# A hybrid block on one core: early sums of the first weight pair, later ring loads and residual adds, output matmuls tied to the last head, and a norm's row that moves

## The chip, the cores and the metric

The kernel runs on one core of a Trainium2 chip. The metric is the device time of one execution in microseconds. The kernel before took 2224.24 us at the median of three runs (2223.49 to 2225.36).

## The reference

One transformer-like block over 512 tokens with a model width of 2048, all in f32:

```
u = rmsnorm(h, attn_norm_w)
z, xbc, dt_raw, q, kc, vc, ks, vs, kw, vw, gate_raw = split(u @ w_in)
y_ssd = ssd_mixer(z, xbc, dt_raw, ...)          # chunked state space, 16 heads
y_att = nsa_mixer(q, kc, vc, ks, vs, kw, vw, gate_raw, ...)   # 16 heads, 4 KV heads
h = h + concat([y_ssd, y_att]) @ w_out
v = rmsnorm(h, ffn_norm_w)
h = h + (silu(v @ w_gate) * (v @ w_up)) @ w_down   # inner width 5632
out = rmsnorm(h, final_norm_w)
```

The attention adds three branches per head: compressed tokens, selected blocks and a window. With 512 tokens there are 8 selection blocks, so every causal block is selected, and the window covers everything too.

## The kernel before, in words

**Precision.** Every operand of a large product is split into a high and a low part: ScalarE casts the high part (`a_hi`, L139), VectorE subtracts it from the f32 value for the low part (`lo`, L142), and TensorE makes three matmuls (a triple) for a pair of operands. A block of weights thus needs a DMA, a cast, a subtract and then its triples.

**Stages.** Times are those of the profiled execution. To about 320 us, `w_in` is read in units (L278 to L280: one unit is a block of 128 columns over k, 512 tokens wide) and the SSD runs beside it. From there to about 770 us the attention heads run, with further units and the first half of `w_out` between them. The attention half of `w_out` follows: columns c=0 and c=1 as units (NOA = 2, `late` for c=1), then c=2 to c=15 as steps (L1419 to L1421) of 8 triples until 857 us. From 857 to 1738 us come 22 pairs of gate and up blocks (NP = 22), each as seven products in the manner of Strassen (M1 to M7). From 1740 us the down product runs in 35 visits (`VISITS`: column group j and a number of pairs n), each with seven products over its n pairs; visits 4 to 13 are at 1773 to 1940 us. The last 56 us are the final norm and the output.

**What orders the work.** The first part is generators under a scheduler that ticks once per triple (`sch.tick`); `yield 10` in a generator waits for ten ticks. Engines run their instructions in the order in which they were issued; `tc.issue_after(x)` pins an instruction behind x. The order of the second part is written out by hand: loads are issued in the order of the list `loads` as soon as slots are free (`advance`, L1331 issues them on SyncE's queue), sums of blocks are made by VectorE (L148), by GpSimd, or by a DMA that accumulates onto the loaded block (`plus`, L1333 on GpSimd's queue), and casts and subtracts run ahead of their triples.

**Places in memory that matter here.** Z and A hold loaded blocks (A has 8 slots), R and E the high and low parts. A lies where attention keeps k, the gates and the split weights of units, so its first writer has to wait until the last unit with attention's output is done. `SR`, a tile inside A's space, held the row of the FFN's norm (`srow`). Columns c=0 and c=1 of `w_out` stand in the list of loads as ghosts: they are not loaded, but take slots in Z.

**Sums for the first pair.** A product needs 11, 12, 22 or one of the sums S1 to S4 of the four blocks of gate (or up). For pair 0 the kernel loads five blocks a side with two accumulating DMAs, and VectorE makes four more sums of 128x1024.

**The ring.** For the down stage the product of gate and up for each pair lies in DRAM in seven forms (`g_d`, 1792 KB a unit), and comes back into a ring of eight slots (GRING = 8). `feed` (L1800 to L1818) issues one load at a time on ScalarE's DMA queue: a whole unit (L1811), or for slot 7 seven pieces of 256 KB (L1814). It issues unit n once `done[n - 8]` lies two steps back, and not faster than one unit per 7 us of the planned time. The first eight units have no predecessor, so they are issued as soon as the pace allows. Units 6 and 7 are first read in visit 8. A DMA of SyncE's or ScalarE's queue signals on one of eight semaphores in turn, and waits for the DMA that used that semaphore last.

**The residual.** h lies in DRAM in eight pieces (`h_d`); `add_h(j)` (L1819) adds piece j onto the output tile of column group j with an accumulating DMA of 512 KB on GpSimd's queue, in visit j+1.

Of the kernel before, what the change touches and what calls it, by code (L numbers as in the profile page):

```python
# [129 lines left out]
def body(ctx, tc, xT, w_in, w_out, w_gate, w_up, w_down, w1k, w1v, cols, rows, kst, out):  # L130
# [38 lines left out]
    def ps_m():  # L169
# [36 lines left out]
    class Unit:  # L206
        def __init__(self, src, nk, rhs, evac, need=(), pre=None, cols=(0, 512)):
            self.cols, self.rhs, self.evac, self.need, self.pre, self.nk = cols, rhs, evac, need, pre, nk
            self.hook, self.late = None, False
# [57 lines left out]
    def run_sub(u, p, sub):  # L267
        i, k0, n = sub
        issue_low(i)
        for j in range(n):  # L270
            if j == 0:
                issue_split(i + LEAD)
            if j == 2:
                issue_low(i + LEAD)
            k = k0 + j
            ah, al = [t[:, u.cols[0]:u.cols[1]] for t in u.rhs(k)]
            with tc.issue_after(R["pv"].ins) if u.late else nullcontext():
                pe.matmul(p, hi_t[i][:, j, :], ah, start=(k == 0), stop=False)  # L278
                pe.matmul(p, hi_t[i][:, j, :], al, start=False, stop=False)  # L279
                pe.matmul(p, lo_t[i][:, j, :], ah, start=False, stop=(k == u.nk - 1))  # L280
            sch.tick()
            if u.hook:
                u.hook(k)
# [368 lines left out]
    def ev_kc(g):  # L652
# [296 lines left out]
    def attention():  # L949
# [45 lines left out]
        def norm2(g, h, br, i):  # L995
            L = 128 * (i + 1)
            e, m = pr[g, h, br, i]
            if not br:
                a_hi(e[:, 0:L], e[:, 0:L], scale=m[:, 3:4])

        def trans(g, h, br, i):
            e, m = pr[g, h, br, i]
# [4 lines left out]
            for kb in range(i + 1):  # L1007
                pe.transpose(p[:, kb * 128:(kb + 1) * 128], e[:, kb * 128:(kb + 1) * 128], ident)
            pr[g, h, br, i] = p[:, 0:128 * (i + 1)].rearrange("p (a b) -> p a b", b=128)
# [9 lines left out]
        def pvmm(g, h, br, i):  # L1019
# [12 lines left out]
            for kb in range(4):  # L1032
                for t in (th, tl):
                    rhs = t[:, 4 * kb:3 * kb + 4, :].rearrange("p a b -> p (a b)")
                    R["pv"] = pe.matmul(o[:, kb * 128:512], v[:, kb, br, :], rhs, start=False,
                                        stop=(br == 1 and kb == 3 and t is tl))
        def out_a(g, h, br, i):
            if br == 1 and i == 3:
# [190 lines left out]
    for c in range(NOA):  # L1229
        units.append(Unit(w_out[c][:, 8:16, :], 8, ma_rhs, ev_head(c)))  # L1230
        units[-1].late = c >= 1

    class Blk:
# [11 lines left out]
        def read(self):  # L1248
            self.reads -= 1
            if not self.reads:  # L1250
                self.zone.free(self.at, self.n)
                self.at = None
# [55 lines left out]
    def advance():  # L1308
        while nxt["raw"] < len(loads):
# [3 lines left out]
            if b.inplace:  # L1313
# [116 lines left out]
    def pre_oa():  # L1430
# [47 lines left out]
    def ev_oa(c):  # L1478
        def ev(p):
# [218 lines left out]
    for u in range(NP):  # L1698
        for side, w in ((0, w_gate), (1, w_up)):
            qs[u, side] = quad(w[u], 0, 8)  # L1700

    loads += [qs[0, side][a] for a, side in (("11", 0), ("11", 1), ("S1", 0), ("12", 0), ("12", 1), ("S1", 1), ("S3", 0),
                                             ("22", 0), ("S3", 1), ("22", 1))]
    seq = [(0, M1), (1, M1), (0, M2), (1, M2), (0, M3), (1, M3)] + [(i, p) for i in range(2) for p in (M6, M7, M5, M4)]
    af0 = {0: gu_after(0, 0), 1: gu_after(0, 1)}
    bk0 = {0: banks(), 1: banks()}
    for n, (side, p) in enumerate(seq):
# [248 lines left out]
    for v, (j, a, b) in enumerate(visits):  # L1956
# [35 lines left out]
        else:  # L1992
            add_loads(q, "11 12 S2 S4 S3 22 S1" if "S4" in made else "11 12 S1 S3 22" if made else "11 12 21 22 S1 S3")
            af, bk = d_after(j, a == 0, b == NP, (j, b) == visits[-1][:2]), banks(BANK_D)
            for n, p in enumerate(SEQ_D):
                blk, sums = q["form"][p]
                s = Step(blk, g_rhs(p, a), bk(p), after=af(p), before=down_before(v, n) if v <= NJ else None, sums=sums)
        done.update((i, s.i) for i in range(a, b))

    def run_rest():  # L2000
# [177 lines left out]
```

## Time and profile before

| what | value |
|---|---|
| median of 3 runs | 2224.24 us |
| profiled execution | 2224.6 us |
| its span | 2222.7 us |
| mean granted TensorE clock | 0.993 |
| TensorE busy | 2172.0 us (98%) |
| VectorE busy | 1771.1 us (80%) |
| ScalarE busy | 1097.8 us (49%) |
| GpSimd busy | 431.1 us (19%) |
| mean DMA rate | 199 GB/s |

All times in the views are from the start of the span. The profile puts an instruction's wait in brackets with what released it; matmuls overlap, so the time between two starts says more than a duration. TensorE is called PE, VectorE DVE, ScalarE ACT, GpSimd POOL and SyncE SP; a q behind the name is that engine's DMA queue.

### The profile page before, as it was taken

What the parts mean: (1) busy time and instruction counts of PE and PEld (TensorE: products, weight loads), DVE (VectorE), ACT (ScalarE), POOL (GpSimd) and SP (SyncE); (2) the same over time, 40 slices, a digit from 0 to 9 for tenths busy, and PEclk for the clock granted to TensorE, in tenths of its full rate; (3) what the DMA queues carried; (4) which work ended last, traced back from release to release, by engine and by line L of the source; (5) the groups of instructions that cost most, each with busy time, mean ns of one, the idle gap of its engine ahead of it and who ended that gap; (6) DMA issues with size and microseconds to landing.
All of it is one profiled execution on the core that took longest, in us unless ns stands there. A gap on an engine that the chain in (4) does not pass through costs nothing. (4 is left out here: it accounts for less than half of the span.)

```text
span 2222.7 us, 39887 instructions
## 1 busy us (share of the span) xinstructions
PE 2172.0 (98%) x15407; PEld 2031.0 (91%) x15407; DVE 1771.1 (80%) x2876; ACT 1097.8 (49%) x1785; POOL 431.1 (19%) x457
## 2 busy tenths in 40 slices
PE   9999999999999899999999999999999999999996
PEld 7888888888888778999999999999999889999996
DVE  6799777788788677888887888888888757787886
ACT  5554457567666544444444444444444443333354
POOL 0012243333133053111111112100000002212121
PEclk9999999999999999999999999999999999999998
DMA  6222443222434176989999999987886988878776
GB/s 204 88 74 67 145 151 105 72 87 84 168 120 149 38 249 165 277 250 260 267 291 264 261 266 265 288 229 222 242 213 217 335 234 260 265 231 274 216 186 175
DMA packets 166607, 442.01 MB, mean 199 GB/s; under 512 B 17952, under 2 KB 32688, under 8 KB 166416
## 3 DMA queue, kind: packets, MB, share of 16 engines
q1 hardware_dynamic: 101872, 256.10, 33.2%
q0 software_dynamic: 32512, 91.73, 21.5%
q10 hardware_dynamic: 32032, 91.63, 11.8%
q8 instruction: 121, 1.98, 0.4%
q14 instruction: 70, 0.57, 0.1%
HBM read 375.95 MB, written 79.63 MB: 205 GB/s over the span
## 5 line engine op out<-in xcount | busy, mean ns | idle before, releaser
L139 ACT ACTIVATE R<-Z 128x1024 fp32r<-128x1024 f32 (+5 forms) x471 | 429.9, 933 | 526.4 <-DVE Z L148 283.3
L142 DVE TENSOR_TENSOR R<-Z,R 128x1024 fp32r<-128x1024 f32 (+5 forms) x365 | 373.9, 1031 | 51.8 <-ACT R L139 38.1
L278 PE MATMUL ps_g<-u,whi 128*128 128x512 f32 x736 | 292.1, 397 | 0.4 <-ACT pth L139 0.4
L280 PE MATMUL ps_g<-u,wlo 128*128 128x512 f32 x736 | 290.4, 395 | 0.0
L279 PE MATMUL ps_g<-u,whi 128*128 128x512 f32 x736 | 289.5, 393 | 0.2 <-DVE u L142 0.2
L1419 PE MATMUL ps_s<-u,R 128*128 128x256 f32 (+1 forms) x753 | 217.3, 289 | 1.7 <-ACT R L139 1.7
L1420 PE MATMUL ps_s<-u,R 128*128 128x256 f32 (+1 forms) x753 | 216.6, 288 | 0.0
L1419 PE MATMUL ps_g<-u,R 128*128 128x256 f32 (+1 forms) x751 | 214.7, 286 | 0.0
L1420 PE MATMUL ps_g<-u,R 128*128 128x256 f32 (+1 forms) x751 | 214.2, 285 | 0.0
L1419 PE MATMUL ps_t<-u,R 128*128 128x256 f32 (+1 forms) x699 | 201.0, 287 | 0.0
L1420 PE MATMUL ps_t<-u,R 128*128 128x256 f32 (+1 forms) x699 | 200.6, 287 | 0.0
L142 DVE TENSOR_TENSOR wlo<-wraw,whi 128x512 fp32r<-128x512 f32 x200 | 156.2, 783 | 49.2 <-ACT whi L139 48.4
L1421 PE MATMUL ps_g<-u,R 128*128 128x256 f32 (+1 forms) x623 | 179.1, 288 | 1.9 <-DVE R L142 1.8
L139 ACT ACTIVATE whi<-wraw 128x512 fp32r<-128x512 f32 x200 | 124.9, 627 | 111.4 <-PE ps_g L279 78.8
L1421 PE MATMUL ps_s<-u,R 128*128 128x256 f32 (+1 forms) x601 | 172.0, 286 | 2.1 <-DVE R L142 2.0
L280 PEld LDWEIGHTS ps_g<-u,wlo 128*128 128x128 f32 x736 | 138.4, 188 | 27.1
L279 PEld LDWEIGHTS ps_g<-u,whi 128*128 128x128 f32 x736 | 138.4, 188 | 26.8 <-DVE u L142 0.5
L278 PEld LDWEIGHTS ps_g<-u,whi 128*128 128x128 f32 x736 | 138.5, 188 | 26.4 <-ACT e L139 0.8
L1419 PEld LDWEIGHTS ps_s<-u,R 128*128 128x128 f32 x753 | 141.6, 188 | 4.1 <-ACT R L139 2.1
L1420 PEld LDWEIGHTS ps_s<-u,R 128*128 128x128 f32 x753 | 142.1, 189 | 2.1
L1420 PEld LDWEIGHTS ps_g<-u,R 128*128 128x128 f32 x751 | 141.8, 189 | 1.5
L1419 PEld LDWEIGHTS ps_g<-u,R 128*128 128x128 f32 x751 | 141.6, 188 | 1.4
(483 smaller groups left out, 6425.7 us busy)
## 6 DMA issues: line engine op xcount, KB each, us to landing
Z<-in_w_gate SPq DMA_DIRECT2D x94, 512.0 KB, 6.7
Z<-in_w_up SPq DMA_DIRECT2D x92, 512.0 KB, 7.3
wraw<-in_w_in SPq DMA_DIRECT2D x164, 256.0 KB, 3.1
g_d<-A ACTq DMA_DIRECT2D x22, 1792.0 KB, 8.1
Z<-in_w_down SPq DMA_DIRECT2D x61, 384.0 KB, 6.9
u<-g_d ACTq DMA_DIRECT2D x11, 1792.0 KB, 9.6
Z<-in_w_gate POOLq DMA_DIRECT2D x35, 512.0 KB, 7.1
Z<-in_w_up POOLq DMA_DIRECT2D x35, 512.0 KB, 6.3
```

What stands on the lines that cost most here:

```text
L139: act.activation(dst, src, AF.Copy, scale=scale)
L142: eng.tensor_tensor(dst, src, f(hi), ALU.subtract)
L278: pe.matmul(p, hi_t[i][:, j, :], ah, start=(k == 0), stop=False)
L279: pe.matmul(p, hi_t[i][:, j, :], al, start=False, stop=False)
L280: pe.matmul(p, lo_t[i][:, j, :], ah, start=False, stop=(k == u.nk - 1))
L1419: pe.matmul(q, h[:, k, :], ah, start=(first and k == 0), stop=False)
L1420: pe.matmul(q, h[:, k, :], al, start=False, stop=False)
L1421: pe.matmul(q, l[:, k, :], ah, start=False, stop=(last and k == n - 1))
```

## The change

It has six parts.

1. **First sums.** A new generator `first_sums` makes S4, S2, S1 and S3 of pair 0, for gate and up, in DRAM: 8 copies of 512 KB on ScalarE's queue and 14 accumulating DMAs on GpSimd's queue, 40 ticks for each part, from the beginning of the scheduler's work on. An accumulate onto a part has to wait for the one before it. The loads of pair 0 are then seven plain ones a side, and the four VectorE adds and four accumulating DMAs at the start of the gate/up stage are gone.
2. **Ring.** `done[-2]` and `done[-1]` are set after visits 4 and 5, so unit 6 is loaded after visit 4 and the pieces of unit 7 after visit 5.
3. **Residual.** `add_h` runs in visits 6 to 13 (at the third product, n == 2), in the order 1, 0, 2 to 7.
4. **Tied output matmuls.** The triples k = 0 to 6 of unit c=0 are pinned behind certain transposes of the last head; k = 7 and unit c=1 stay behind its last matmul.
5. **The norm's row** is made in place in `rrow`, which does not lie in A.
6. **Ghosts** take no slots in Z.

The core of the diff:

```diff
+            if k in u.pins:
+                sch.run_until(("pin", u.pins[k]))
+                pin = R["pin", u.pins[k]]
+            elif u.late:
+                pin = R["pv"]
+            with tc.issue_after(pin.ins) if pin else nullcontext():
...
+    def first_sums():
+        terms = {"S1": ("21", "22"), "S3": ("21", "11"), "S2": ("21", "22", "11"), "S4": ("21", "22", "11", "12")}
+        parts = [(s0_d[side, a], [w[0][int(t[0]) - 1, int(t[1]) - 1] for t in terms[a]])
+                 for a in ("S4", "S2", "S1", "S3") for side, w in ((0, w_gate), (1, w_up))]
+        yield 4
+        for n in range(len(parts) + 3):
+            if n < len(parts):
+                tc.keep_in_program_order(nc.scalar.dma_start(parts[n][0], parts[n][1][0]))
+            for d in (3, 2, 1):
+                yield 10
+                if 0 <= n - d < len(parts) and d < len(parts[n - d][1]):
+                    tc.keep_in_program_order(nc.gpsimd.dma_start(parts[n - d][0], parts[n - d][1][d], accum_op=ALU.add))
+            yield 10
...
+        if c == 0:
+            units[-1].pins = dict(enumerate([(3, 3, 0, 2), (3, 3, 0, 2), (3, 3, 1, 0), (3, 3, 1, 0), (3, 3, 1, 2), (3, 3, 1, 3), (3, 3, 1, 3)]))
...
+            if b.ghost:
+                b.at = 0
+                nxt["raw"] += 1
+                continue
...
-        yield from rms_stats(rrow, D, P2["srow"], "s", keep=True, gap=2)
+        yield from rms_stats(rrow, D, rrow, "s", keep=True, gap=2)
...
+            qs[u, side] = quad(w[u], 0, 8, made={} if u else {a: s0_d[side, a] for a in ("S1", "S2", "S3", "S4")})
...
-            if n == 4 and 0 < v <= NJ:
-                assert v > 1 or not any(fz.busy[NZ2:])
-                add_h(v - 1)
+            if (v, n) == (1, 4):
+                assert not any(fz.busy[NZ2:])
+            if n == 2 and v > 5:
+                add_h([1, 0, 2, 3, 4, 5, 6, 7][v - 6])
...
+        if v in (4, 5):
+            done[(6 if v == 4 else 7) - GRING] = s.i
...
+    sch.add(first_sums())
```

In the rows below, lines of the kernel after are shifted by the added ones (L278 to L286, L1008 to L1034, L1811 to L1842, L1814 to L1845).

TensorE near the end of attention, before: the triples of unit c=0 (`ps_g<-u`, k up to 5) end, and scores of the heads (`kh`, `kl`) and transposes (`ident,e`) follow.

```order
L279 MATMUL ps_g<-u,whi 128x512
L280 MATMUL ps_g<-u,wlo 128x512
L278 MATMUL ps_g<-u,whi 128x512
L279 MATMUL ps_g<-u,whi 128x512
L280 MATMUL ps_g<-u,wlo 128x512
L965 MATMUL ps_s<-kh,rq 128x128
L966 MATMUL ps_s<-kl,rq 128x128
L965 MATMUL ps_s<-kh,rq 128x256
L966 MATMUL ps_s<-kl,rq 128x256
L1008 MATMUL ps_t<-ident,e 128x128 x5
```

The same engine in the last head, after: transposes, the compressed branch (`cph`, `cpl`), transposes again.

```order
L1034 MATMUL ps_t<-ident,e 128x128 x5
L286 MATMUL ps_g<-u,whi 128x512
L287 MATMUL ps_g<-u,whi 128x512
L288 MATMUL ps_g<-u,wlo 128x512
L286 MATMUL ps_g<-u,whi 128x512
L287 MATMUL ps_g<-u,whi 128x512
L288 MATMUL ps_g<-u,wlo 128x512
L1054 MATMUL ps_s<-cph,vpad 128x512
L1055 MATMUL ps_s<-cpl,vpad 128x512
L1034 MATMUL ps_t<-ident,e 128x128 x5
L286 MATMUL ps_g<-u,whi 128x512
```

Six triples of that unit stood in front of these scores; now two stand behind each group of five transposes, and the others further on in the same head.

GpSimd in the SSD, before: products for the skip term (`t`, `xt`) and the running state (`pf`).

```order
L145 TENSOR_TENSOR t_1541<-xt,rowc 128x512
L148 TENSOR_TENSOR xt<-xt,t_1608 128x512
L145 TENSOR_TENSOR t_1907<-xt,rowc 128x512
L145 TENSOR_TENSOR t_2052<-xt,rowc 128x512
L145 TENSOR_TENSOR pf<-pf,decb 128x512
L148 TENSOR_TENSOR xt<-xt,t_2119 128x512
```

The same place after, with the accumulating DMAs (`s_d0...` and `s_d1...` are the parts in DRAM):

```order
L145 TENSOR_TENSOR t_1557<-xt,rowc 128x512
L148 TENSOR_TENSOR xt<-xt,t_1624 128x512
L686 DMA s_d1S_103<-in_w_up 128x1024
L686 DMA s_d0S_100<-in_w_gate 128x1024
L145 TENSOR_TENSOR t_1928<-xt,rowc 128x512
L686 DMA s_d1S_104<-in_w_up 128x1024
L686 DMA s_d1S_103<-in_w_up 128x1024
L686 DMA s_d0S_100<-in_w_gate 128x1024
L145 TENSOR_TENSOR t_2074<-xt,rowc 128x512
L145 TENSOR_TENSOR pf<-pf,decb 128x512
L148 TENSOR_TENSOR xt<-xt,t_2142 128x512
```

Two accumulates stand ahead of one product of the second group, three ahead of the next.

ScalarE in visits 3 and 4, before: casts (L139), evacuations (L1852 to L1859), the load of unit 6 (L1811) and pieces of unit 7 (L1814).

```order
L139 ACTIVATE R<-E_18378 128x512
L1811 DMA u<-g_d 128x4x896
L139 ACTIVATE R<-E_18378 128x512
L139 ACTIVATE R<-Z 128x512
L1852 ACTIVATE A<-ps_t 128x512
L139 ACTIVATE R<-Z 128x512 x2
L139 ACTIVATE R<-Z 128x640 x2
L1858 ACTIVATE A<-ps_s 128x512
L1859 ACTIVATE A<-ps_s 128x256
L1814 DMA V_8471<-g_d 128x512
L139 ACTIVATE R<-Z 128x640
L1814 DMA T<-g_d 128x512
```

ScalarE in visit 5 (casts of 128x768), after:

```order
L139 ACTIVATE R<-Z 128x768
L1883 ACTIVATE A<-ps_s 128x512
L1842 DMA u<-g_d 128x4x896
L139 ACTIVATE R<-Z 128x768 x3
L139 ACTIVATE R<-E_18404 128x768
L1889 ACTIVATE A<-ps_g 128x512
L1890 ACTIVATE A<-ps_g 128x256
L139 ACTIVATE R<-Z 128x768
L139 ACTIVATE R<-E_18404 128x768
L139 ACTIVATE R<-Z 128x768
L1883 ACTIVATE A<-ps_t 128x512
L1845 DMA V_8501<-g_d 128x512
```

Unit 6 is asked for in visit 5, behind the casts of its first products, and the first piece of unit 7 where the casts for visit 6 are under way.

More of the change, by code (lines that the diff above doesn't have):

```diff
@@ L177, in body @@
     sl_d = dram.tile([2, 128, 9, 128], F32, name="sl_d")[:, :, 0:8, :]
+    s0_d = {(side, a): dram.tile([128, 9, 128], F32, name=f"s0_d{side}{a}")[:, 0:8, :]
+            for side in range(2) for a in ("S4", "S2", "S1", "S3")}
     h1_d = dram.tile([KD, 128, 512], F32, name="h1_d")
@@ L208, in __init__ @@
             self.cols, self.rhs, self.evac, self.need, self.pre, self.nk = cols, rhs, evac, need, pre, nk
-            self.hook, self.late = None, False
+            self.hook, self.late, self.pins = None, False, {}
             self.sub = []
@@ L276, in run_sub @@
             ah, al = [t[:, u.cols[0]:u.cols[1]] for t in u.rhs(k)]
-            with tc.issue_after(R["pv"].ins) if u.late else nullcontext():
+            pin = None
+            if k in u.pins:
[4 more added lines that the diff above has]
+            with tc.issue_after(pin.ins) if pin else nullcontext():
                 pe.matmul(p, hi_t[i][:, j, :], ah, start=(k == 0), stop=False)
@@ L999, in norm2, with pin_at @@
                 a_hi(e[:, 0:L], e[:, 0:L], scale=m[:, 3:4])
+        def pin_at(what, ins):
+            R["pin", what] = ins
+            sch.flags.add(("pin", what))
         def trans(g, h, br, i):
@@ L1007, in trans @@
             for kb in range(i + 1):
-                pe.transpose(p[:, kb * 128:(kb + 1) * 128], e[:, kb * 128:(kb + 1) * 128], ident)
+                x = pe.transpose(p[:, kb * 128:(kb + 1) * 128], e[:, kb * 128:(kb + 1) * 128], ident)
+            pin_at((g, h, br, i), x)
             pr[g, h, br, i] = p[:, 0:128 * (i + 1)].rearrange("p (a b) -> p a b", b=128)
@@ L1036, in pvmm @@
                                         stop=(br == 1 and kb == 3 and t is tl))
+                    pin_at((g, h, br, "pv", kb, t is tl), R["pv"])
         def out_a(g, h, br, i):
@@ L1249, in read @@
             self.reads -= 1
-            if not self.reads:
+            if not self.reads and not self.ghost:
                 self.zone.free(self.at, self.n)
@@ L1699, in body @@
         for side, w in ((0, w_gate), (1, w_up)):
-            qs[u, side] = quad(w[u], 0, 8)
-    loads += [qs[0, side][a] for a, side in (("11", 0), ("11", 1), ("S1", 0), ("12", 0), ("12", 1), ("S1", 1), ("S3", 0),
-                                             ("22", 0), ("S3", 1), ("22", 1))]
+            qs[u, side] = quad(w[u], 0, 8, made={} if u else {a: s0_d[side, a] for a in ("S1", "S2", "S3", "S4")})
+    loads += [qs[0, side][a] for a in ("11", "12", "S4") for side in range(2)]
+    loads += [qs[0, side][a] for side in range(2) for a in ("S2", "S3", "S1", "22")]
     seq = [(0, M1), (1, M1), (0, M2), (1, M2), (0, M3), (1, M3)] + [(i, p) for i in range(2) for p in (M6, M7, M5, M4)]
@@ L1996, in body @@
                 blk, sums = q["form"][p]
-                s = Step(blk, g_rhs(p, a), bk(p), after=af(p), before=down_before(v, n) if v <= NJ else None, sums=sums)
+                s = Step(blk, g_rhs(p, a), bk(p), after=af(p), before=down_before(v, n) if v < NJ + 6 else None, sums=sums)
         done.update((i, s.i) for i in range(a, b))
+        if v in (4, 5):
+            done[(6 if v == 4 else 7) - GRING] = s.i
     def run_rest():
```

5 lines of the change are left out of this document (1 added, 4 removed).

## Prediction

> **What bounds the kernel now.** I read the busy time by stretches first. Its columns are the stretch, its length, then busy us (and instructions) of TensorE, its weight loads, VectorE, ScalarE and GpSimd, the granted TensorE clock, the DMA share and GB/s.
>
> ```profile
> 700.00:800.00 100.00, 92.87 (x456) 75.44 (x455) 69.34 (x181) 56.35 (x130) 22.79 (x24) 0.97 0.36 117
> 800.00:900.00 100.00, 96.52 (x562) 84.94 (x561) 81.15 (x97) 47.72 (x60) 37.02 (x45) 0.98 0.69 201
> 900.00:1700.00 800.00, 799.16 (x6753) 798.75 (x6752) 660.27 (x745) 358.09 (x401) 107.80 (x124) 1.00 0.90 254
> 1700.00:1800.00 100.00, 88.68 (x701) 86.12 (x700) 73.71 (x112) 44.22 (x77) 3.46 (x4) 0.97 0.85 296
> ```
>
> TensorE bounds nearly everything: in 900 to 1700 it misses 0.84 of 800 us. An edit pays only where it waits or runs at a lower clock, and the three other stretches show such places: 7.1, 3.5 and 11.3 us idle. Clock losses come on top, so I counted instructions. In the next rows the undisturbed 1800:1860 gives 60.00/510 = 0.1176 us per matmul of a step.
>
> ```profile
> 860.00:882.00 22.00, 18.52 (x145) 18.11 (x144) 18.51 (x20) 12.60 (x16) 6.02 (x6) 0.92 0.48 124
> 1740.00:1760.00 20.00, 16.23 (x125) 14.99 (x125) 17.61 (x39) 12.70 (x30) 1.73 (x2) 1.00 1.00 338
> 1776.00:1800.00 24.00, 17.04 (x113) 16.34 (x114) 13.12 (x18) 8.11 (x13) 0.86 (x1) 0.86 0.82 289
> 1800.00:1860.00 60.00, 60.00 (x510) 60.00 (x509) 43.20 (x54) 25.97 (x38) 10.45 (x10) 1.00 0.86 242
> ```
>
> At that pace 145 instructions take 17.1 of 22 us (4.9 lost at the start of the gate/up stage), 125 take 14.7 of 20 (5.3 lost at the start of the down stage) and 113 take 13.3 of 24 (10.7 lost in visit 4). The change aims at the first and the third of these, at the end of attention and at the handover behind it; the 5.3 us I leave alone, since VectorE is busy there for 17.61 of 20 us and nothing of its work is removed.
>
> **Part 1, the output matmuls among the last transposes.**
>
> ```profile
> 737.00:741.00 4.00, 4.00 (x20) 3.28 (x19) 4.00 (x11) 2.87 (x8) 1.84 (x2) 1.00 0.00 0
> 741.00:757.00 16.00, 14.32 (x87) 11.60 (x86) 12.76 (x52) 12.39 (x36) 1.03 (x1) 1.00 0.05 17
> 757.00:770.05 13.05, 9.81 (x44) 7.08 (x42) 6.90 (x19) 5.66 (x15) 0.00 (x0) 0.74 0.26 82
> ...
> 737.10 0.40 PE L279 MATMUL ps_g<-u,whi 128*128 128x512 f32 x1
> 740.75 0.39 PE L280 MATMUL ps_g<-u,wlo 128*128 128x512 f32 x1
> 760.53 1.13 PE L1008 MATMUL ps_t<-ident,e 128*128 128x128 f32 x5 [1.23 <-DVE ptl L142]
> 762.14 0.79 PE L1035 MATMUL ps_s<-pth,v 128*128 128x512 f32 x1 [0.47 <-ACT pth L139]
> 762.86 0.79 PE L1035 MATMUL ps_s<-ptl,v 128*128 128x512 f32 x1
> ```
>
> Of unit c=0, k0 to k5 stood ahead of 741: 18 matmuls at 0.228 us (16 of them from 737.10 to 740.75), 4.1 us. They now fill bubbles of the last head. In 757:770.05 TensorE was idle for 13.05 - 9.81 = 3.2 us, and a granted clock of 0.74 cost 0.26 x 9.81 = 2.6 us: the two 512-wide matmuls at 762.14 and 762.86 start 0.72 apart. Taking 4.1 us out ahead of 741 uncovers VectorE: it was busy 4.00 of 4.00 us before 741, and 12.76 of 16 behind it, so only 3.2 us of slack can take up the 4.1. I expect some 2 us of new waits in 741:757, most of the 3.2 us of bubbles filled, and the clock held: about -2.7. The bounds are -0.5 (VectorE has no room, clock as before) and -5.0 (nearly all of 3.2 + 2.6).
>
> By the Trainium skill, "TensorE: Matmul & The Clock Gate", section "HAM oscillation", the rule is no TensorE gap over about 3.4 us; bubbles of 1.2 us would then cost no clock, and the clock's 2.6 us would not be there to win. The trace disagrees with the rule as put: the longest shown wait in 757:770.05 is 1.23 us and the clock fell. By the rule alone the term would be -0.1 and the total 2.6 us higher; I keep the trace's.
>
> **Part 2, the norm's row out of A, and ghost blocks without Z slots.** TensorE's waits, then ScalarE and the load queue:
>
> ```profile
> 776.00 0.39 PE L280 MATMUL ps_g<-u,wlo 128*128 128x512 f32 x1
> 778.08 0.50 PE L1419 MATMUL ps_s<-u,R 128*128 128x512 f32 x1 [1.69 <-ACT R L139]
> 779.34 0.50 PE L1421 MATMUL ps_s<-u,E 128*128 128x512 f32 x1 [0.53 <-DVE E L142]
> ...
> 776.49 0.60 ACT L348 ACTIVATE A<-ps_m 128x512 f32<-128x512 f32 x1 [4.25 <-PE ps_g L280]
> 776.98 2.00 ACT L139 ACTIVATE R<-Z 128x1024 fp32r<-128x1024 f32 x2
> ...
> 756.72 0.81 SPq L1331 DMA_DIRECT2D Z<-in_w_out  x2
> 776.42 0.33 SPq L1331 DMA_DIRECT2D A<-in_w_out  x1
> ```
>
> The copy of the row into A could start only when the last head had left A's space, at 776.49, and ScalarE, in order, held the cast of the first w_out block behind it. That block was asked for at 756.72. With the row elsewhere the copy stands earlier, the cast and VectorE's subtract run under the 6.2 us of output matmuls, and the loss goes: from 776.23 (776.00 and one 0.23 step) to 779.34 there are 3.1 us for two matmuls, so 2.6 lost. Next late would be a block that goes into A, asked for at 776.42; with the ghost blocks holding no slots, four blocks instead of two go to Z at once, 4 x 24 matmuls of 0.23 us, 22 us of work. I take -2.4; bounds -1.5 and -2.6.
>
> **Part 3, sums of the first pair made early.**
>
> ```profile
> 867.91 0.38 PE L1421 MATMUL ps_s<-u,R 128*128 128x256 f32 x1 [0.61 <-DVE R L142]
> 873.88 0.58 PE L1421 MATMUL ps_t<-u,E 128*128 128x256 f32 x1 [2.88 <-DVE E L142]
> ...
> 864.25 2.47 DVE L148 TENSOR_TENSOR Z<-Z 128x1024 f32<-128x1024 f32 x2
> 870.21 1.22 DVE L148 TENSOR_TENSOR Z<-Z 128x1024 f32<-128x1024 f32 x1
> 871.46 1.22 DVE L148 TENSOR_TENSOR A<-A,Z 128x1024 f32<-128x1024 f32 x1
> 872.60 1.22 DVE L142 TENSOR_TENSOR E<-Z,R 128x1024 fp32r<-128x1024 f32 x1
> ```
>
> Four adds of 1.22 us leave VectorE. The 2.88 us wait ends on the subtract at 872.60, which stood behind two of them; the 0.61 us wait ends on one that stood behind the pair at 864.25. Without them those subtracts come 2.4 us sooner or more, the clock need not recover, and of 4.9 us I take back 4.3. What is left: VectorE still has one subtract and one other 1.22 us piece per step of 24 x 0.1176 = 2.82 us. Bounds -2.5 and -5.2.
>
> Its price lies earlier: 8 copies on ScalarE's queue and 14 accumulating DMAs on GpSimd's, between GpSimd's operations for the SSD. Those of before there, VectorE's read of the second, and the landing of such an accumulate (KB, us):
>
> ```profile
> 195.13 1.38 POOL L145 TENSOR_TENSOR t<-xt,rowc 128x512 f32<-128x512 f32 x1
> 202.40 3.16 POOL L145 TENSOR_TENSOR t<-xt,rowc 128x512 f32<-128x512 f32 x1 [5.89 <-DVE xt L148]
> 209.72 0.42 DVE L148 TENSOR_TENSOR t<-ps_t,t 128x256 f32<-128x256 f32 x1
> ...
> Z<-in_w_gate POOLq DMA_DIRECT2D x35, 512.0 KB, 7.1
> ```
>
> Two accumulates now stand ahead of the first, three ahead of the second, and an accumulate onto a block waits for the one before it, 7.1 us at the median. The second has room: it ends at 205.56 and is read at 209.72, and it had idled 5.89 us ahead. I take +0.5, bounds -0.5 (no reason for a gain beyond scatter) and +4 (most of one landing on the chain).
>
> **Part 4, ring loads after visits 4 and 5.** TensorE's three waits, the chain of waits, ScalarE, and the load's group (KB, median us):
>
> ```profile
> 1777.44 0.38 PE L1421 MATMUL ps_s<-V,R 128*128 128x256 f32 x1 [1.71 <-DVE R L142]
> 1779.96 0.39 PE L1421 MATMUL ps_s<-V,R 128*128 128x256 f32 x1 [0.48 <-DVE R L142]
> 1788.53 0.58 PE L1419 MATMUL ps_t<-V,R 128*128 128x256 f32 x1 [4.97 <-ACT R L139]
> ...
> 1763.08 24.27 DMA u<-g_d
> ...
> 1787.37 0.33 ACTq L1814 DMA_DIRECT2D u<-g_d  x1
> 1787.74 0.74 ACT L139 ACTIVATE R<-Z 128x640 fp32r<-128x640 f32 x1 [8.18 <-DMA u<-g_d]
> ...
> u<-g_d ACTq DMA_DIRECT2D x11, 1792.0 KB, 9.6
> ```
>
> Unit 6 was issued at 1763.08, between stretches at 338 and 289 GB/s, and took 24.27 us instead of 9.6; unit 7's fourth piece, next on its semaphore, held ScalarE's queue until 1787.35, and the cast behind it came 8.18 us late. Nothing reads unit 6 before visit 8. Loaded after visit 4, it leaves 3.6 MB out of the crowded stretch, and the pieces come a visit (126 matmuls, 14.8 us) behind it, longer than 9.6. The 4.97 us wait goes with its slow matmuls, and the 1.71 and 0.48 us waits (a sum's load from DRAM, late in the same traffic) shrink. Of 10.7 us I take -9.5; bounds -6 (the late sum stays) and -11.2 (with what the neighbouring rows lose).
>
> **Part 5, residual adds at visits 6 to 13,** eight accumulating DMAs of 512 KB from GpSimd, one a visit: five leave visits 1 to 5, five come to 9 to 13, and the same traffic arriving later, with GpSimd's sums of `w_down` blocks queued behind each issue. The adds themselves wait less there: each adds onto a block written five visits earlier or more, where before it came one visit behind. What they find: 242 GB/s in 1800:1860 against 338 in 1740:1760. With the 3.6 MB that arrive in the 30 us of visits 5 and 6 it is 242 + 120 = 362 for a while, less the adds that left. I take +1.0 for both, bounds 0 and +4.
>
> **Sum:** -2.7 - 2.4 - 4.3 - 9.5 + 0.5 + 1.0 = -17.4. The profiled execution took 2224.6 us (span 2222.7, 1.9 around it), 0.4 above the median of 2224.24: 2207.2 on its own scale, 2206.8 on the median's. All bounds at their worst give -0.5 - 1.5 - 2.5 - 6 + 4 + 4 = -2.5, at their best -24.5.
>
> **Rivals.**
> *The ring's wait moves with the loads.* Visits 5 and 6 then carry the 362 GB/s worked out above. For it: between 338 and 289 GB/s a load took 24.27. Against it: that holds for some 30 us only, and the adds of visits 4 and 5 are gone from it. If unit 6 is that late again, a piece holds ScalarE for 24.27 - 15 = 9 us, as the 8.18 did, and TensorE pays about 5.1 of the 9.5: 2211.9. Chance 0.14.
> *DMA bandwidth is the bound, and moved bytes are paid wherever they go.* Visits 4 to 13 then get no faster as a whole, term 4 is paid back bit by bit, and 2206.8 + 9.5 = 2216.3 comes out. For it: DMA shares of 1.00 and 0.86 in 1740:1760 and 1800:1860. Against it: 242 GB/s in the latter is far under 338 in the former, so there is room to move into. Chance 0.06. The Trainium skill's page "Trainium Kernel Development and Optimization", section "Key Constraints", has this rule: the queues of all engines share the same 16 DMA engines, and issuing from another saves issue time alone.
> *VectorE takes all of part 1.* The 4.1 us come back as waits in 741:757 and the clock stays low: the term is 0, the time 2209.5. For it: 4.00 of 4.00 us. Chance 0.06.
> *Slower: GpSimd's queue blocks in the SSD.* If each accumulate waits for its predecessor's landing, 14 x 7.1 = 99 us of GpSimd's queue stand ahead of `t` and `xt` operations, whose slack is 4.2 us at 205.56. It decides once over 17.9 us of it reach TensorE (the other terms' sum), and shows from 22.3; with a quarter, 25 us, the time is 2206.3 + 25 = 2231. Against it: ticks space an accumulate from its predecessor. Chance 0.04.
>
> **How the numbers follow.** The forecast gets 0.70: 2206.8, own range 2201 to 2212. Two in ten may be left out; the range takes in the first and third rival and leaves out the second, the fourth and the forecast's tails: 2201 to 2214. 0.2%, 4.4 us, is about what a measurement of this kernel can tell from no change: same is 2219.8 to 2228.7. Faster takes forecast and three rivals, less a remainder for losses that no row shows: 0.92; same 0.04, slower 0.04.
>
> **What would show it.** Right: no ScalarE wait on `u<-g_d` in visit 4 and 113 instructions there in some 14 us; no VectorE wait of over 1 us in the first twelve us of gate/up; the first w_out matmul within 0.3 us of the last output matmul; a granted clock over 0.9 in the last head. Wrong: a 5 us wait in visits 5 to 7 (first rival), a DMA share near 1 through visit 13 with waits on `Z<-in_w_down` (second), no shorter 737:770 (third), TensorE idle for several us between 190 and 260 on VectorE or GpSimd (fourth).

## The result and the profile after

The kernel after took 2211.57 us at the median of six runs (2209.92 to 2214.48), the kernel before 2223.86 (2221.83 to 2225.36) beside it: a ratio of 0.9944, with an interval from 0.9935 to 0.9954. That is 12.3 us less, where 17.4 were forecast. 2211.57 lies at the upper end of the forecast's own range and within 0.4 of what the first rival would have given, so the time alone doesn't tell them apart; the rows below do. The profiled execution of the kernel after took 2212.1 us (span 2210.2).

The instructions of TensorE are the same in both kernels up to small changes of order, so the start of the n-th middle matmul of a triple (L279 and L1420 before, L287 and L1454 after) can be set side by side. All of these matmuls are in the traces, 4613 in each kernel. The difference, after less before, at nine places (a gain between two places is the difference of two rows):

| start before, us | place | start after, us | difference | change since the row above |
|---|---|---|---|---|
| 289.28 | amid the compression | 290.67 | +1.4 | +1.4 |
| 361.59 | compression done | 367.47 | +5.9 | +4.5 |
| 712.10 | ahead of the last heads | 719.34 | +7.2 | +1.4 |
| 793.24 | third `w_out` step | 793.05 | -0.2 | -7.4 |
| 877.28 | gate/up, first pair | 871.84 | -5.4 | -5.3 |
| 1733.80 | end of gate/up | 1728.14 | -5.7 | -0.2 |
| 1801.42 | visit 5 | 1784.67 | -16.8 | -11.1 |
| 1941.60 | end of visit 13 | 1928.83 | -12.8 | +4.0 |
| 2201.53 | last visit | 2189.54 | -12.0 | +0.8 |

Between visit 5 and 1854.67 us the difference stays at -16.75: nothing is lost in visits 5 to 8.

The busy time by stretches of the kernel after shows the two places that the change aimed at, with the columns as before:

```profile
860.00:882.00 22.00, 22.00 (x188) 22.00 (x187) 17.71 (x22) 15.04 (x18) 4.60 (x4) 1.00 0.69 217
1760.00:1784.00 24.00, 24.00 (x206) 24.00 (x205) 18.37 (x26) 12.83 (x21) 0.00 (x0) 1.00 0.56 182
1860.00:1930.00 70.00, 65.66 (x533) 63.42 (x532) 45.72 (x63) 22.91 (x30) 14.98 (x13) 1.00 0.90 282
```

The start of the gate/up stage holds 188 matmuls in 22 us where it held 145, and the 24 us around visits 3 and 4 hold 206 where 1776:1800 held 113: full pace, at a granted clock of 1.00. The third row is the new loss: 533 in 70 us, some 7 us short of the pace. The kernel before, at the same times but some 15 us less far in its work, had 562, some 4 us short:

```profile
1860.00:1930.00 70.00, 67.83 (x562) 66.40 (x560) 50.64 (x68) 25.94 (x33) 10.65 (x8) 1.00 0.83 265
```

The last head of the kernel after, by stretches, then on TensorE, then on ScalarE:

```profile
745.00:760.00 15.00, 12.57 (x74) 9.07 (x73) 14.19 (x54) 13.18 (x37) 2.85 (x3) 1.00 0.05 18
760.00:773.00 13.00, 12.89 (x72) 10.62 (x73) 8.37 (x26) 7.43 (x21) 0.00 (x0) 1.00 0.48 163
```

```profile
768.08 0.73 PE L1034 MATMUL ps_t<-ident,e 128*128 128x128 f32 x5
768.57 0.47 PE L286 MATMUL ps_g<-u,whi 128*128 128x512 f32 x1
...
771.30 0.40 PE L1062 MATMUL ps_s<-pth,v 128*128 128x512 f32 x1
771.54 0.46 PE L1062 MATMUL ps_s<-ptl,v 128*128 128x512 f32 x1
...
778.56 0.39 PE L288 MATMUL ps_g<-u,wlo 128*128 128x512 f32 x1
778.79 0.39 PE L1453 MATMUL ps_s<-u,R 128*128 128x512 f32 x1
```

```profile
774.68 3.90 ACT L139 ACTIVATE R<-Z 128x1024 fp32r<-128x1024 f32 x4
```

The pinned triples fill the last head (12.89 of 13.00 us busy, two 512-wide matmuls 0.24 us apart instead of 0.72), and VectorE now bounds the stretch ahead of it: 14.19 of 15 us, with 2.4 us of idle time on TensorE (1.7 in 741:757 of the kernel before). The first step's matmul at 778.79 stands 0.23 behind the last output matmul, since ScalarE had cast four blocks from 774.68 on.

The loss ahead of 362 us: GpSimd's queue, the load issued at 296.64 (KB, us to landing), ScalarE and TensorE of the kernel after.

```profile
295.85 0.92 POOL L686 DMA_DIRECT2D s_d0S<-in_w_gate  x1
296.64 0.72 POOL L722 DMA_DIRECT2D w1r<-in_w1v  x1
299.06 0.55 POOL L722 DMA_DIRECT2D w1r<-in_w1v  x1 [1.70 <-DVE w1l L142]
307.90 0.54 POOL L722 DMA_DIRECT2D w1r<-in_w1v  x1 [8.29 <-DVE xr L732]
...
w1r<-in_w1v POOLq DMA_DIRECT2D x1, 256.0 KB, 9.5
```

```profile
306.25 0.63 ACT L139 ACTIVATE w1h<-w1r 128x512 fp32r<-128x512 f32 x1 [5.67 <-DMA w1r<-in_w1v]
...
306.93 0.38 PE L740 MATMUL ps_s<-w1h,xh 128*124 128x256 f32 x1 [1.69 <-ACT w1h L139]
```

An accumulating DMA of the first sums stands among the loads of the compression weights (`w1r`); it took 9.3 us to land. The load behind it, issued 0.8 us later at 296.64, took 9.5 us (nine of these sixteen loads take 3.0 to 3.6; the two in the same place in the kernel before took 6.0 and 5.3) and landed at 306.15. ScalarE waited 5.67 us for it and TensorE 1.69. In the kernel before such a cast never kept TensorE waiting. The rest of the 4.5 us between 289 and 362 is smaller waits of this kind and one step of 3.4 us at half the clock, at 323.8, which costs 1.7.

### The profile page after: what moved, and what is told of

It is laid out like the page before. It is cut to its first block, busy times and chain, and to the rows that moved or that the text cites. A ratio compares the mean times of both kernels' runs of the same rounds, so it can differ in the third digit from the quotient of the medians.

```text
span 2210.2 us, 39923 instructions
## 1 busy us (share of the span) xinstructions
PE 2168.1 (98%) x15407; PEld 2026.3 (92%) x15407; DVE 1767.7 (80%) x2872; ACT 1096.4 (50%) x1785; POOL 435.7 (20%) x467
## 5 line engine op out<-in xcount | busy, mean ns | idle before, releaser
L139 ACT ACTIVATE R<-Z 128x1024 fp32r<-128x1024 f32 (+5 forms) x479 | 435.2, 929 | 507.1 <-DVE Z L148 256.2
L142 DVE TENSOR_TENSOR R<-Z,R 128x1024 fp32r<-128x1024 f32 (+5 forms) x400 | 416.9, 1049 | 52.5 <-ACT R L139 39.3
L286 PE MATMUL ps_g<-u,whi 128*128 128x512 f32 x736 | 293.0, 398 | 1.5 <-DVE h L145 1.5
L287 PE MATMUL ps_g<-u,whi 128*128 128x512 f32 x736 | 290.2, 394 | 0.0
L1454 PE MATMUL ps_s<-u,R 128*128 128x256 f32 (+1 forms) x753 | 216.6, 288 | 0.0
L1454 PE MATMUL ps_g<-u,R 128*128 128x256 f32 (+1 forms) x751 | 214.1, 285 | 0.0
L1454 PE MATMUL ps_t<-u,R 128*128 128x256 f32 (+1 forms) x699 | 199.9, 286 | 0.0
L139 ACT ACTIVATE whi<-wraw 128x512 fp32r<-128x512 f32 x200 | 124.6, 626 | 111.5 <-PE ps_g L287 75.9
L286 PEld LDWEIGHTS ps_g<-u,whi 128*128 128x128 f32 x736 | 138.8, 189 | 27.3 <-issue 1.9
L287 PEld LDWEIGHTS ps_g<-u,whi 128*128 128x128 f32 x736 | 138.9, 189 | 26.4
L1454 PEld LDWEIGHTS ps_s<-u,R 128*128 128x128 f32 x753 | 142.2, 189 | 2.2
L1454 PEld LDWEIGHTS ps_g<-u,R 128*128 128x128 f32 x751 | 141.6, 189 | 1.5
```

The source lines that it names most:

```text
L139: act.activation(dst, src, AF.Copy, scale=scale)
L142: eng.tensor_tensor(dst, src, f(hi), ALU.subtract)
L1454: pe.matmul(q, h[:, k, :], al, start=False, stop=False)
```

## The experiments

All ratios are against the kernel before in the same series of runs. The kernel after was run again in one of them: 2213.34 us, 0.9955 (0.9941 to 0.9969), with TensorE's wait for the compression weights there once more (2.0 us) and no slow clock behind it. The table gives, for the profiled execution of each kernel, the difference to the kernel before at the places above.

| kernel | median, us | ratio (interval) | 289 | 362 | 712 | 793 | 877 | 1734 | 1801 | 1942 | 2202 |
|---|---|---|---|---|---|---|---|---|---|---|---|
| after | 2211.57 | 0.9944 (0.9935 to 0.9954) | 1.4 | 5.9 | 7.2 | -0.2 | -5.4 | -5.7 | -16.8 | -12.8 | -12.0 |
| after, again | 2213.34 | 0.9955 (0.9941 to 0.9969) | 2.7 | 5.6 | 5.9 | -0.3 | -5.6 | -6.4 | -17.5 | -12.9 | -12.3 |
| no early sums | 2216.69 | 0.9969 (0.9957 to 0.9982) | 0.6 | 2.2 | 1.9 | -3.5 | -4.1 | -5.5 | -16.6 | -8.5 | -8.2 |
| copies only | 2219.79 | 0.9978 (0.9965 to 0.9991) | 1.0 | 6.3 | 16.3 | 8.3 | 3.0 | 5.8 | -5.3 | -0.9 | 0.0 |
| sums later | 2213.83 | 0.9955 (0.9940 to 0.9971) | 1.2 | 2.7 | 6.9 | -0.6 | -5.8 | -5.5 | -16.6 | -11.0 | -10.5 |
| adds back | 2208.79 | 0.9937 (0.9916 to 0.9959) | 1.6 | 7.9 | 9.7 | 2.3 | -3.0 | -4.0 | -15.1 | -13.4 | -12.8 |
| ring lines undone | 2212.24 | 0.9949 (0.9933 to 0.9964) | 1.8 | 4.0 | 5.3 | -2.2 | -7.5 | -8.5 | -19.6 | -13.7 | -11.9 |
| ring undone, adds back | 2217.35 | 0.9971 (0.9960 to 0.9981) | 2.4 | 5.4 | 6.4 | 0.1 | -5.2 | -4.9 | -8.6 | -6.9 | -6.5 |
| ring lines alone, on before | 2219.40 | 0.9983 (0.9974 to 0.9993) | 0.3 | 0.4 | 0.1 | 0.9 | 0.6 | -0.4 | -8.7 | -8.0 | -7.2 |
| row back in A | 2216.94 | 0.9970 (0.9961 to 0.9979) | 1.6 | 5.3 | 5.0 | 1.6 | -3.7 | -1.3 | -12.3 | -7.6 | -7.0 |
| no pins | 2215.88 | 0.9973 (0.9961 to 0.9986) | 2.1 | 7.0 | 11.3 | 11.1 | 5.8 | 4.4 | -6.7 | -2.2 | -1.5 |
| fast sums, adds back | 2205.90 | 0.9922 (0.9907 to 0.9936) | 2.4 | 1.1 | 1.1 | -3.1 | -8.4 | -9.7 | -20.8 | -18.7 | -17.7 |

One profile shows one execution; where it is far from its kernel's median, the text says so. Steps of halved clock fall in different places in different executions (last section); 6.8 us of them cost 3.4, and the text names those that matter for a difference.

**No early sums.**

```diff
-    sch.add(first_sums())
...
-            qs[u, side] = quad(w[u], 0, 8, made={} if u else {a: s0_d[side, a] for a in ("S1", "S2", "S3", "S4")})
+            qs[u, side] = quad(w[u], 0, 8)
```

The order of the loads and the sums of pair 0 are those of the kernel before again.

> The kernel after without part 3 of the prediction (early sums): pair 0 again with VectorE adds and accumulating loads. Between the kernels before and after, the difference of equal matmuls grew by 5.8 us up to 322 us and shrank by some 5 us at the start of the gate/up stage. Theory: the copies and accumulating DMAs cause the 5.8 us by themselves. Then this run is back to before's pace up to 322 us (0 to 0.5 us behind) and loses 4.4 to 5.3 us at the gate/up start: 2211.6 - 5.8 + 5 = about 2210.8. Rival: the 5.8 us come from another part that changes the order there (the tied matmuls, the ring): then this run is still 5 us late at 322 and takes about 2216.5.

At 362 us this kernel is 2.2 us behind, not 5.9. Both have one step of halved clock there (1.6 of the 2.2), so the sums cost 3.7 us, most of the early loss. At the gate/up start it gains 0.6 us where the kernel after gains 5.3. Without the sums 4.7 us are thus lost there and 3.7 saved before, +1.0, yet the time rose by 3 to 5. In the profile 8.1 us, not 4.0, go again between visit 5 and visit 14; 3.4 of that is the granted clock, halved for 6.8 us at 1873.6. What makes the medians differ by more than +1.0 is open.

**Copies only.** The 14 accumulating DMAs are left out; the sums of pair 0 keep their first terms.

```diff
-                if 0 <= n - d < len(parts) and d < len(parts[n - d][1]):
+                if False:
```

> The kernel after with the 8 copies but without the 14 accumulating DMAs (the sums of pair 0 are left out, the first terms stand in their place). Theory that the accumulates on GpSimd's queue cost the early time: up to 322 us this run is within 1 us of before, and it keeps the gain at the gate/up start: 2211.6 - 5 = about 2206.5. Rival that the copies do it, or any early traffic: 3 us or more of the 5.8 stay, 2209.5 or more.

By its numbers the rival came out: 6.3 us behind at 362, and 2219.79. But the loss is of another kind. Up to 313 us this kernel is at most 1.2 us behind, where the kernel after is 3.9; then the granted clock is halved for 10.2 us at 318.9, behind small waits of 0.33 to 0.36 us, and that alone costs 5.1. No load of the compression weights takes over 7.0 us (in the kernel after two take 8.1 and 9.5), and ScalarE's longest wait for one is 2.4, not 5.67, which fits the theory. ScalarE's waits for them in total are as long as in the kernel after, though (14.5 against 14.0 us), so not all of those are due to the accumulates. 10 us more go up to 712, where the scheduler had put the heads in another order. As the order of TensorE differs from that of the kernel after from 200 to 755 us, the time of this run doesn't tell what the accumulates cost.

**Sums later.**

```diff
     def first_sums():
...
+        yield from sch.wait("cmp")
```

> The kernel after with the same copies and accumulating DMAs, begun only once the compressed tokens are done (about 320 us), beside the attention heads, where the DMA share is about 0.3. Theory that their collision with the SSD's GpSimd operations and with the loads of the compression weights (258 to 322 us) costs the 5.8 us: it goes, and 2211.6 - 5 = about 2206.5 comes out. Rival that accumulates cost time wherever GpSimd has work (attention keeps it a third busy): the loss moves into 330 to 640 us and the time stays within 1.5 of 2211.6.

The rival is nearer: at 362 us the loss is 2.7 instead of 5.9 (1.7 of it a step of halved clock at 320.0), but 4.2 us go between 362 and 712, where the kernel after loses 1.4. The time is that of the kernel after within the intervals (0.9955).

**Adds back.**

```diff
-            if n == 2 and v > 5:
-                add_h([1, 0, 2, 3, 4, 5, 6, 7][v - 6])
+            if n == 4 and 0 < v <= NJ:
+                add_h(v - 1)
```

> The kernel after with the residual adds back in visits 1 to 8. In the kernel after, 4 us of the gain were lost again in visits 9 to 13. Theory: the adds that now stand there cost them, in GpSimd's queue and in traffic ahead of the weight sums. Then visits 9 to 13 lose under 1 us here, and visits 1 to 5 lose 1 to 3 us again: the time is 2209 to 2211.6. Rival: the loads of units 6 and 7 and the missing stall behind them bring the payback; then visits 9 to 13 still lose about 4 us against before and the time is 2211.6 or more.

The theory came out in the profile, and better: between visits 5 and 14 1.7 us go instead of 4.0, and visits 0 to 5 gain 11.1 us as they did without the adds. The median, of four runs, is 2.8 us under the kernel after (4.6 under its second run); the intervals of the ratios overlap, so the rows below carry the reading. GpSimd's queue at 1886 us shows the mechanism. The kernel after, its queue and its group of accumulating loads (KB, median us to landing):

```profile
1886.33 0.87 POOL L1850 DMA_DIRECT2D A<-h_d  x1
1886.91 1.18 POOL L1367 DMA_DIRECT2D Z<-in_w_down  x1
...
Z<-in_w_down POOLq DMA_DIRECT2D x4, 384.0 KB, 6.9
```

The kernel with the adds back:

```profile
1886.77 0.87 POOL L1367 DMA_DIRECT2D Z<-in_w_down  x1
...
Z<-in_w_down POOLq DMA_DIRECT2D x4, 384.0 KB, 4.9
```

The load of a block that is summed by accumulating is issued 0.6 us behind the add in GpSimd's queue and lands after 6.9 us instead of 4.9. Its cast and its subtract are late, once a visit. These waits are new, in the kernel after alone:

```profile
1878.51 0.39 PE L1455 MATMUL ps_g<-u,R 128*128 128x256 f32 x1 [0.31 <-DVE R L142]
1895.71 0.39 PE L1455 MATMUL ps_s<-u,R 128*128 128x256 f32 x1 [0.22 <-DVE R L142]
1912.37 0.39 PE L1455 MATMUL ps_t<-u,R 128*128 128x256 f32 x1 [0.36 <-DVE R L142]
1928.49 0.39 PE L1455 MATMUL ps_g<-u,R 128*128 128x256 f32 x1 [0.45 <-DVE R L142]
```

All waits of TensorE from 1860 to 1945 add up to 4.3 us, in the kernel with the adds back to 2.7. The first four moved adds, at 1803.81 to 1852.32, are issued behind their load and not ahead of it, and up to 1854.67 nothing is lost. One of them, in the kernel after, with the landing of the add and of the load:

```profile
1820.36 0.86 POOL L1367 DMA_DIRECT2D Z<-in_w_down  x1
1820.94 1.17 POOL L1850 DMA_DIRECT2D A<-h_d  x1
...
A<-h_d POOLq DMA_DIRECT2D x1, 512.0 KB, 8.7
Z<-in_w_down POOLq DMA_DIRECT2D x1, 384.0 KB, 4.9
```

Here the load keeps its 4.9 us, and the add, for which TensorE doesn't wait, takes the longer time. So the order of the two seems to cost, more than the bytes; no run puts the last four adds behind their loads.

**Ring lines undone.**

```diff
-        if v in (4, 5):
-            done[(6 if v == 4 else 7) - GRING] = s.i
```

> The kernel after without the two lines that hold back units 6 and 7: they are asked for as in the kernel before, with the adds still in visits 6 to 13. Theory (prediction, part 4): the early load alone made the wait of 5 us, so the 9 to 10.8 us between 1740 and 1797 us come back: some 2211.6 + 10 less the 4 us of payback in visits 9 to 13, if those came from the earlier arrival; 2217 to 2222. Rival: the five adds that left visits 1 to 5 had freed the stretch; then unit 6 lands in time without the ring lines, the 5 us wait stays away, and the time is within 2 us of 2211.6.

The rival came out: 11.1 us are gained up to visit 5 without these lines, and the time is that of the kernel after. Unit 6, asked for at 1754.53, landed in 13.4 us: without the adds of visits 1 to 4 the stretch had room. Later this kernel gives back more (-19.6 to -13.7 at visit 14); why is open.

**Ring undone and adds back.** Both edits above in one kernel.

> The kernel after with both the ring lines undone and the residual adds back in visits 1 to 8. With one of the two undone, visits 3 to 5 stayed 11.1 us shorter than before. Theory: unit 6 is late only if its load and the adds of visits 1 to 4 meet in that stretch, so that either edit alone is enough; with both undone the 24 us landing, the 5 us wait and the slow clock come back, 9 to 11 us, and the time is 2208.8 + 10 = about 2219. Rival: something else in the change (four more loads and eight more copies shift which DMAs share a semaphore) had removed the wait; then it stays away here too, and the time is 2208 to 2212.

The theory came out, somewhat smaller than expected. The chain of waits, TensorE and ScalarE of this kernel:

```profile
1758.13 22.70 DMA u<-g_d
```

```profile
1782.06 0.58 PE L1453 MATMUL ps_g<-V,R 128*128 128x256 f32 x1 [3.71 <-ACT R L139]
```

```profile
1781.28 0.74 ACT L139 ACTIVATE R<-E 128x640 fp32r<-128x640 f32 x1 [6.30 <-DMA u<-g_d]
```

Unit 6 takes 22.70 us again, ScalarE waits 6.30 for it and TensorE 3.71. Against the kernel with only the adds back it loses 7.4 us up to visit 5 (-3.7 instead of -11.1; 3.71 of wait and 6.8 us of halved clock behind it, 3.4) and 8.6 at the median. So the load of unit 6 and the adds are late together, and either edit alone takes the wait away. The rival has a share too: TensorE's waits of 1.71 and 0.48 us for a late sum, ahead of the long one in the kernel before, are gone here as well, 2.8 us in all. The load of that sum went out at 1753.91 and took 10.4 us; in the kernel before, at 1760.79, it took 14.9. Neither the ring lines nor the moved adds did that, and which other part did is open.

**Ring lines alone, on the kernel before.** The two lines above added to it.

> The kernel before with the two ring lines alone. Theory: this is the largest part by itself: visits 3 to 5 are 10 to 11 us shorter, and under 2 us are given back in visits 9 to 13, since the adds stay in visits 1 to 8: 2223.9 - 9 = about 2215. Rival: the loads moved behind visit 4 only push the wait to visits 6 to 8: over 4 us are given back there, and the time is 2219 or more.

The time is the rival's (2219 or more), but its mechanism isn't there: in the profile nothing is given back in visits 5 to 8, and 0.7 by visit 14. 8.3 us are gained up to visit 5, the 4.97 us wait and the 3.4 us of slow clock behind it. The late sum still costs what it did:

```profile
1777.08 0.39 PE L1421 MATMUL ps_s<-V,R 128*128 128x256 f32 x1 [1.80 <-DVE R L142]
```

That execution was the fastest of ten (2217.49), while the profiled one of the kernel before was 1.8 us above the median beside this run. At the medians the lines bring 3.4 us (0.9974 to 0.9993). The 3.4 us of clock needn't be lost in every execution of the kernel before, which may be part of this; no other of its executions was profiled, and the difference is open.

**Row back in A.**

```diff
-        yield from rms_stats(rrow, D, rrow, "s", keep=True, gap=2)
+        yield from rms_stats(rrow, D, P2["srow"], "s", keep=True, gap=2)
...
```

The lines left out give `srow` its place in A again and let the norm read it there.

> The kernel after with the norm's row back in the space of A (ghost blocks still without slots). Theory (prediction, part 2): the cast of the first w_out block again stands behind the row's copy, and 2.4 to 2.7 us come back at the handover: about 2214. Rival: four loads at once and earlier are what mattered, or other slack hides the copy: within 1 us of 2211.6, no wait of ScalarE's row ahead of the first step.

The theory came out at the handover. ScalarE, then TensorE:

```profile
778.09 0.60 ACT L356 ACTIVATE A<-ps_m 128x512 f32<-128x512 f32 x1 [4.26 <-PE ps_g L288]
778.59 3.90 ACT L139 ACTIVATE R<-Z 128x1024 fp32r<-128x1024 f32 x4
```

```profile
779.69 0.50 PE L1453 MATMUL ps_s<-u,R 128*128 128x512 f32 x1 [1.69 <-ACT R L139]
780.95 0.50 PE L1455 MATMUL ps_s<-u,E 128*128 128x512 f32 x1 [0.53 <-DVE E L142]
```

The casts stand behind the copy again, and the waits of 1.69 and 0.53 us are those of the kernel before, though four blocks were there to be cast at once: the ghosts alone don't take the wait away. No run takes part 6 out by itself. From 712 to 793 us this kernel gains 3.4; the kernel after in its second profile, which had the same 3.4 us of halved clock there, gains 6.2: the row is worth 2.8. The time, 2216.94, is 3 us above the expected one; in the profile 2.4 us go between 877 and 1734, 1.7 of them in a step of halved clock at 1230.3, and the rest of that excess is open.

**No pins.**

```diff
-            units[-1].pins = dict(enumerate([(3, 3, 0, 2), (3, 3, 0, 2), (3, 3, 1, 0), (3, 3, 1, 0), (3, 3, 1, 2), (3, 3, 1, 3), (3, 3, 1, 3)]))
```

> The kernel after without the pins of unit c=0's triples (k = 0 to 6). Theory (prediction, part 1): the bubbles of the last head are back, with a slow clock in some executions; 3 to 5 us come back before the first w_out step: 2215 to 2217. Rival: VectorE bounds that stretch with or without the pins (14.19 of 15 us busy in 745 to 760 of the kernel after); then under 1.5 us come back.

The theory came out: 2.5 to 4.3 us at the medians against the two runs of the kernel after. The profile is of the slowest of ten executions (2222.56): from 712 to 793 it gains 0.2 us, not 7.4. The waits of the last head are back as they were before (1.22, 0.47, 0.29 and 0.69 us), and the granted clock was halved for 13.7 us there, which is 6.8 of the 7.2 us. So the price of the bubbles is mostly the clock, and it differs from execution to execution. Its stretch:

```profile
772.00:785.70 13.70, 12.25 (x39) 9.20 (x38) 5.46 (x13) 4.79 (x9) 0.00 (x0) 0.50 0.25 94
```

**Fast sums, adds back.** Adds in visits 1 to 8, and 28 ticks a part instead of 40:

```diff
-                yield 10
+                yield 7
...
-            yield 10
+            yield 7
```

> The kernel after with the residual adds in visits 1 to 8 (as in the first run of them, 2208.8) and the first sums made at 28 ticks a part instead of 40, so that they are done when the loads of the compression weights begin. Theory: the wait for those loads (1.7 us in the kernel after, 3.6 in the run with the adds back) and the slow clock behind it go, some 4 us: 2204 to 2206. Rival: closer spacing makes the accumulates wait for each other in GpSimd's queue, ahead of the SSD's products, and the loss only moves to 120 to 250 us: 2208 or more.

The theory came out, and this kernel has the lowest median: 2205.90 us, 0.9922, its interval clear of that of the kernel after in the same series (from 0.9941). It is 1.1 us behind at 362 instead of 5.9, though one accumulate still falls beside the compression weights. What ScalarE waited for them, in the kernel after and then here (in total, times, longest):

```profile
ACT w1h L139 <- DMA w1r<-in_w1v: 9.2, 5, 5.7
ACT w1h L139 <- DMA w1r<-in_w1k: 4.8, 3, 2.0
```

```profile
ACT w1h L139 <- DMA w1r<-in_w1k: 1.7, 2, 0.9
ACT w1h L139 <- DMA w1r<-in_w1v: 1.2, 1, 1.2
```

14.0 us became 2.9, and TensorE waits for none of it; the longest of these loads took 7.1 us instead of 9.5.

## Why the prediction was right, and where it was not

The time lay in the range, and the likeliest case was the one that happened: TensorE has no wait at the start of the gate/up stage, the first step follows the last output matmul by 0.23 us, ScalarE no longer waits for unit 6, and no long wait came up in visits 5 to 7. But two prices that I had put at +0.5 and +1.0 came to some 4 to 5 and +4, and the early loss was 7.2 us at 712. That the total is off by 5 us and not by 10 is luck: the gains came out 4.9 us larger than forecast, 2.3 in parts 1 and 2, 1.0 in part 3 and 1.6 in part 4.

- **Parts 1 and 2** were forecast at -2.7 and -2.4; together 7.4 us were won from 712 to 793 us. The row's 2.8 is the forecast, a little over its bound of -2.6. The pins won the rest, 4.6 in that execution. The last head's idle time fell from 3.2 to 0.1 us, and ahead of it VectorE took back 0.9 us (2.6 us idle from 719 to 760 where 1.7 were before), not the 2 expected. Some 3 us of the gain are the clock, which was halved for 6.8 us at 760.7 in the kernel before. It held in that execution of the kernel after; in the second one it was halved for 3.4 us at 747.1. (The prediction's row of 16 matmuls from 737.10 to 740.75 has 17; its 0.228 us per matmul and its 4.1 us stand.)
- **Part 3's gain** is -5.3 in the profile against -4.3; the kernel without the sums still gains 0.6 there, so the sums bring 4.7.
- **Part 3's price is the step that failed most:** "I take +0.5, bounds -0.5 (no reason for a gain beyond scatter) and +4". I had priced the accumulates only against the SSD's products. There they cost about 1 us (1.4 at 289 us). But 11 rounds of 40 ticks are some 300 us, so the generator reaches past the SSD to the loads of the compression weights, which use the same queue, and one accumulate ahead of one load made TensorE wait. The early loss is 5.9 us with the sums and 2.2 without, a price of 3.7. Against the kernel before with only the ring lines (0.4) it is 5.5, but 1.6 of that is a step of the clock. That the place of the accumulates matters is shown by the kernel with fast sums, which is 1.1 behind.
- **Part 4** was forecast at -9.5 and measured at -11.1, within its bound. 8.3 of it is the mechanism that was forecast, unit 6 late in a crowded stretch, and that is shown. The other 2.8 are the late sum, which the prediction let shrink with the traffic; the kernel with the ring lines alone still pays it and the one with both edits undone doesn't, so that part of the number is luck. That the ring lines win the 8.3 is only half of it, too. Without them the moved adds win it, and the prediction had booked the adds' leaving as nothing.
- **Part 5's +1.0** became +4.0, its upper bound; 2.3 of that go with the adds (4.0 against 1.7). The step that failed is "What they find: 242 GB/s": it looked at bandwidth, not at the place of one add in GpSimd's queue, directly ahead of a load that the next cast waits for. Given the ring lines, part 5 brings nothing in visits 0 to 5 (11.1 us either way) and costs those 2.3; the medians agree (2208.79 without it), though not clear of noise.
- **The rivals.** No wait moved with the ring loads (the difference stands still through visits 5 to 8). Bandwidth as the bound of visits 4 to 13 is refuted: as a whole they got 7.1 us shorter (-5.7 to -12.8), and in the adds-back run, with the adds in visits 1 to 8 again, 9.4. VectorE did not take all of part 1. GpSimd's queue did block in the SSD, for 2.6 and 1.7 us, far from the 17.9 that would have decided.

The Trainium skill's rule in "TensorE: Matmul & The Clock Gate", section "HAM oscillation", of no gap over some 3.4 us, does not cover what was seen; the last section shows the rows.

## What to carry to other kernels

Before you move a stream of DMAs to a quiet stage, work out how long the stream lasts and what it meets at its far end, and look at what stands behind each piece in its queue: a load that a cast waits for loses more by one place in the queue than the bandwidth shows. An add that isn't needed soon can stand behind that load, as the first four moved adds did here. Where two transfers are late together, undo them one at a time and together, since either edit alone may win everything and the second then only costs.

## What the runs showed of the hardware

**The clock drops in steps of about 3.4 us, and not always behind the same waits.** In the kernel after, a stretch behind the waits at the end of compression:

```profile
320.40:323.80 3.40, 1.74 (x29) 1.22 (x28) 1.36 (x3) 1.24 (x4) 0.00 (x0) 1.00 0.51 165
323.80:327.20 3.40, 3.40 (x10) 2.66 (x10) 1.51 (x5) 3.17 (x8) 3.14 (x7) 0.50 0.15 28
```

In the kernel before, the same waits (1.74 of 3.40 us busy in both) and the stretch behind them:

```profile
316.00:319.40 3.40, 1.74 (x29) 1.19 (x28) 1.29 (x4) 1.24 (x4) 0.00 (x0) 1.00 0.44 144
319.40:322.80 3.40, 3.40 (x22) 2.84 (x19) 1.56 (x5) 3.00 (x8) 2.94 (x6) 1.00 0.16 34
```

The longest wait in either is 1.0 us. The granted clock was then 0.50 for one such step in the one and 1.00 in the other: 10 instructions of TensorE against 22. In the kernel with fast sums it was 0.50 for three steps, in the middle of the heads, where no single wait was over 0.7 us:

```profile
742.70:752.90 10.20, 10.20 (x41) 9.53 (x41) 7.69 (x28) 6.89 (x18) 1.03 (x1) 0.50 0.02 8
```

The Trainium skill's "TensorE: Matmul & The Clock Gate", section "Part 1: The HAM clock gate", has the clock at full or half by windows of 3413 ns that run on their own and do not start with the work. The traces agree with both. In the kernel before, the stretches of halved clock ahead of the final norm start at 648.09, 760.73, 873.37 and 1788.14 us, which lie 33, 33 and 268 times 3.413 us apart, and each lasts 3.413 us or twice that. In every other profile they lie on such a grid too, at another distance from the start of the span. What follows for measuring such a kernel: a change that leaves a stage alone can still move it against these windows, by 1.7 us a step (half of 3.4; in the kernel without early sums the difference grew by 1.6 us over its step at 320.5). That is the size of several differences above, and likely much of the scatter: of 25 executions of the kernel before in one series, the three with a mean granted clock of 0.991 or less took 2226.5 to 2228.1 us, the three at 0.995 took 2218.7 to 2220.2.

**Of two DMAs close together in GpSimd's queue the second was the one that took longer.** A 384 KB accumulating load issued 0.6 us behind a 512 KB add took 6.8 to 7.1 us, without the add 4.8 to 5.0; the add ahead of it took 5.2 to 5.5, as alone. With the load ahead, at 1820.36, it took 4.9 and the add 8.7. A 256 KB load issued 0.8 us behind a 512 KB accumulate took 9.5 us, where nine of the sixteen of its kind took 3.0 to 3.6; that accumulate, with other loads in flight, took 9.3.
